# Two hybrid blocks on one core: narrow attention products given all of TensorE's rows, meta values taken once per head pair, and the squares of a norm gathered in one tile

## The chip, the cores and the metric

The kernel runs on one core of a Trainium2 chip. A core has five engines that run side by side, each working through its own instructions in order: TensorE (PE, matrix products; its weight loads are listed as PEld), VectorE (DVE), ScalarE (ACT), GpSimd (POOL) and SyncE (SP), which here only issues DMAs. They wait for each other by semaphores. Products go to PSUM, a small memory that is given out here in eight banks of 128 x 512 numbers; everything else lies in SBUF, 128 partitions wide. A matrix product takes a stationary operand of up to 128 rows by 128 columns and streams a moving one of up to 512 columns through it; the rows are the partitions over which it sums. The metric is the time of the whole program on the device in microseconds; lower is better.

## The reference, cut to what matters

Two transformer-like blocks run one after the other on 512 tokens of width 1024, all in 32-bit floats. The first block has a recurrent branch (a state-space model in chunks), an attention branch and a feed-forward part; the second a gated recurrent branch and a latent attention. The change touches both attentions and the norms:

```python
# first block: 16 heads of 64 in 2 key groups; a band of 128 keys and 16 meta tokens
s_band = einsum('bnqkgd,bnskd->bnkgqs', qb, kband) * scale + bias_band
s_meta = einsum('bnqkgd,bmkd->bnkgqm', qb, k_meta) * scale + bias_m
p = softmax(concatenate([s_meta, s_band, sink], -1), -1)
out = (einsum('bnkgqm,bmkd->bnqkgd', p_meta, v_meta)
       + einsum('bnkgqs,bnskd->bnqkgd', p_band, vband))
# second block: 8 heads, keys of 128 own numbers and 64 rotated ones that all heads share
s = (einsum('bqhd,bkhd->bhqk', qn, k_nope)
     + einsum('bqhr,bkr->bhqk', qp, k_pe)) * scale
# every norm
y = x * rsqrt(mean(x * x, axis=-1) + EPS)
```

## The kernel before, in words

**Layout.** Activations lie transposed: channels on the partitions, tokens in the free dimension. A weight tile of 128 x 1024 arrives by one DMA of 512 KB (`wload`), ScalarE copies it to a shortened form (`whi`, type fp32r) and VectorE takes the rest (`wlo`). The activations are split likewise (`split_hl`). A product of two such pairs is three products, high by high, high by low and low by high (`gemm`, lines 88 to 90), on 128 rows, in half-tokens of 256 to 264 columns in the first block and in 512 columns in the second.

**First block.** `first_mixer` goes over four groups of the recurrent branch. Each has a tile of B, one of C, four tiles x and four z; `pair_a` and `pair_b` work on a pair of heads. While a group runs, the convolution tiles of the next group (`conv_tile`, the list `jobs`), and in the last group the keys, values and queries of the attention, are put between the pairs, and so are the four output tiles of the group before (`branch`, the list `br`). `group_end` sums the squares of the group that is finished and makes the row of its norm.

**Its attention.** `attention` works on eight pairs of heads, one head of each key group on 64 partitions. `kx` is the keys laid out for four blocks of 128 queries (144 columns for the first, 272 for the others, the 16 meta keys among them). `kh[k]` holds the high part of head k's keys on both halves of the partitions, `qx[k]` the high part of its queries on one half and the low part on the other, so that one product of 128 rows (line 596) gives high by high and low by high. The third, high by low, is line 597: 64 rows of `qx` and the same 64 of `kl`, which holds the low parts of both heads, one above the other. VectorE adds the bias and takes the maximum out of PSUM (line 598), ScalarE the exponential, VectorE the scaling. `values` turns the weights round by transposes (lines 621, 633 and 637), and collects the output in one PSUM bank `pv`: for each of four query blocks first the meta values (line 640: `vm`, 32 rows, of both heads, by 128 columns), then the bands (lines 644 and 645, 64 columns of output for each head). After every head pair `self.fill` puts in other projections.

**Second block.** `Block2.run` first makes the gated recurrent branch (`hgrn_a`, `hgrn_b`), between whose heads it puts the list `jobs` of `lora_jobs`: two tiles of the key latent and three of the query latent, each with squares for its norm. Then eight heads of attention: `mla_split` divides keys and queries into high and low, `mla_a` projects the next head's, `mla_b` makes scores, softmax and transposes, `mla_c` the values. In `mla_b` the 64 rotated numbers come as one product of 128 rows (line 1137: `qx` has high and low query parts, `kph` the high key part on both halves) and one of 64 rows (line 1138: the high query part by `kpl`, the low key part). Which half of `qx` holds the high part depends on the head being even or odd. Line 1139 adds the causal mask.

**Sums of squares.** `SumSq` takes tile after tile. ScalarE squares (line 153). From the third on, the second of two kept tiles is added to the first by POOL (line 147), before a new square is made, so that two are left at the end, and `sums` (line 163) sums both over the partitions by products with a column of ones, each in two passes. There are nine such norms (four groups, the feed-forward's, two at the start of the second block, two latents) and a closing one, which is taken in two halves.

**Order.** The program text gives each engine's work; the framework's scheduler, which runs its own estimate of the engines, lays the final order of each engine's instructions and gives out buffers (a tile with the same tag waits for the earlier ones of that tag, `bufs` at a time). PSUM has tags g, a, t and o with 3, 2, 2 and 1 banks in the first block and the feed-forward, 2, 3, 2 and 1 in the second.

Of the kernel before, what the change touches and what calls it, by code (L numbers as in the profile page):

```python
# [12 lines left out]
F32 = mybir.dt.float32  # L13
F32R = mybir.dt.float32r
# [4 lines left out]
ALU = mybir.AluOpType  # L19
# [114 lines left out]
class SumSq:  # L134


    def __init__(self, g, pool, rows, nchunk, ntok, tag="ssq", bufs=1, sqtag="sq", sqbufs=2):
        self.g, self.pool, self.rows, self.nchunk, self.ntok = g, pool, rows, nchunk, ntok
        self.tag, self.bufs, self.sqtag, self.sqbufs = tag, bufs, sqtag, sqbufs
        self.parts = []  # L140

    def add(self, src, scale=None):
        nc = self.g.nc
        w = self.rows * self.nchunk
        if len(self.parts) == 2:
            a, sq = self.parts
            nc.gpsimd.tensor_tensor(a[:, :self.ntok], a[:, :self.ntok], sq[:, :self.ntok], ALU.add)  # L147
            self.parts = [a]
        tag, bufs = (self.sqtag, self.sqbufs) if self.parts else (self.tag, self.bufs)
        sq = self.pool.tile([128, w], F32, name="sq", tag=tag, bufs=bufs)  # L150
        if w > self.ntok:
            nc.gpsimd.memset(sq[:, self.ntok:], 1.0)
        nc.scalar.activation(sq[:, :self.ntok], src, AF.Square, **({} if scale is None else {"scale": scale}))  # L153
        self.parts.append(sq)

# [53 lines left out]
class Mixer:  # L209
# [288 lines left out]
    def attention(self, wk, nfill):  # L498
# [4 lines left out]
        kx = wk.tile([128, 960], F32, name="kx", tag="kx")  # L503
# [9 lines left out]

        half = (slice(0, 64), slice(64, 128))
        kh = [wk.tile([128, 960], F32R, name=f"kh{k}", tag=f"kh{k}") for k in range(2)]
        kl = wk.tile([128, 960], F32R, name="kl", tag="kl")
        for k in range(2):
            r = half[k]
            nc.scalar.activation(kh[k][r, :], kx[r, :], AF.Copy)
            nc.vector.tensor_tensor(kl[r, :], kx[r, :], kh[k][r, :].bitcast(F32), ALU.subtract)  # L520
            nc.vector.tensor_copy(kh[k][half[1 - k], :], kh[k][r, :].bitcast(F32))
# [51 lines left out]
        def scores(j):  # L573
# [17 lines left out]
            for b in range(4):  # L591
                for k in range(2):
                    n = 272 if b else 144
                    keys, cols = slice(KO[b], KO[b + 1]), slice(b * 128, (b + 1) * 128)
                    ps = psum(g, "a")
                    nc.tensor.matmul(ps[:, :n], qx[k][:, cols], kh[k][:, keys], start=True, stop=False)
                    nc.tensor.matmul(ps[:, :n], qx[k][half[k], cols], kl[half[k], keys], start=False, stop=True)  # L597
                    nc.vector.tensor_tensor_reduce(
                        out=lay(b, k), in0=ps[:, :n], in1=(bias if b else bias0)[:, k, :], scale=1.0,
                        scalar=sink[:, 2 * j + k:2 * j + k + 1], op0=ALU.add, op1=ALU.max, accum_out=mx[:, b, k:k + 1])  # L600
# [14 lines left out]
        def values(j, s):  # L615
# [8 lines left out]
            pv = psum(g, "o")  # L624
            for b in range(4):
# [14 lines left out]
                nc.tensor.matmul(pv[:, cols], vm, ptm[:, cols], start=(b == 0), stop=False)  # L640
# [39 lines left out]
def first_mixer(g, h1):  # L680

    nc, tc = g.nc, g.tc
    with ExitStack() as ctx:
# [4 lines left out]
        with tc.tile_pool(name="ssd", bufs=1, side="right", reuse_waits="tile") as wk, \  # L688
# [6 lines left out]
            for gi in range(4):  # L695
# [5 lines left out]
                for i in range(4):  # L701
                    parts = m.pair_a(wk, gi, i)
                    if prev:
                        m.pair_b(wk, *prev)
                        if i == 0:
                            br = m.group_end(wk, gi - 1)
                    prev = (gi, i, parts)
                    k = (len(jobs) + 3 - i) // (4 - i) if gi == 3 else (2 if jobs else 0)
                    m.fills = jobs[:k] + br[:1]
                    jobs, br = jobs[k:], br[1:]  # L710
                    m.fill(99)
# [99 lines left out]
class Block2:  # L811
# [191 lines left out]
    def lora_jobs(self):  # L1003
# [3 lines left out]
        self.lat, self.rl, self.mz = {}, {}, {}  # L1007

        def part(name, first, i, n, gname):
            if i == 0:  # L1010
                self.lat[name] = []
                self.ss = SumSq(g, self.wk, 128, 4, NX, "ssqa", 1, "ssqb", 1)
            t = self.t("lt")
            self.mulR(t, self.win(first + i), self.R)
# [5 lines left out]
            if i == n - 1:  # L1020
                self.rl[name] = self.ss.rstd(128.0 * n, gname)

        def kpe():
# [6 lines left out]
            self.kpe = (self.t("R1", dt=F32R, name="kph"), self.t("lt", dt=F32R, name="kpl"))  # L1030
            split_hl(g, k, *self.kpe)
# [15 lines left out]
        self.gate = gate  # L1047
        return j, kpe, norm
# [55 lines left out]
    def mla_split(self, h, kn, qn):  # L1104
# [7 lines left out]
        pr = slice((h % 2) * 64, (h % 2) * 64 + 64)  # L1112
        pl = slice(64 - (h % 2) * 64, 128 - (h % 2) * 64)
        nc.scalar.activation(qx[pr, :], qpe[pr, :], AF.Copy)
        nc.vector.tensor_tensor(qx[pl, :], qpe[pr, :], qx[pr, :].bitcast(F32), ALU.subtract)
        return kn2, qn2

    def mla_b(self, h, parts):
# [4 lines left out]
        pr = slice((h % 2) * 64, (h % 2) * 64 + 64)  # L1123
# [6 lines left out]
        def soft(b):  # L1130
# [7 lines left out]
            nc.tensor.matmul(ps[:, :n], qx[pr, qs], kpl[pr, :n], start=False, stop=False)  # L1138
# [37 lines left out]
    def run(self, r1, r12):  # L1176
# [6 lines left out]
        for h in range(8):  # L1183
# [9 lines left out]
            if 1 <= h < 6:  # L1193
                jobs.pop(0)()
# [11 lines left out]
    def output(self):  # L1206
# [30 lines left out]
        ssq = [SumSq(g, self.wk, 128, 2, HN, f"at{i}", 1, ("o", "ki")[i]) for i in range(2)]  # L1237
# [266 lines left out]
```

## Time and profile before

| what | value |
|---|---|
| median of 3 runs | 1845.95 us (1844.37 to 1847.08) |
| the profiled execution | 1847.94 us, its span 1846.1 us |
| TensorE busy, weight loads | 1802.4 us (98%), 1611.1 us (87%) |
| VectorE, ScalarE, POOL busy | 1134.4, 749.3, 299.4 us |
| granted TensorE clock | 0.994 of full |
| DMA | 158.35 MB, mean 86 GB/s |

The span is the time from the first to the last instruction of one profiled execution; the timed runs are without a profile. A row of the order of time has the start, the duration (both us), the engine, the line, the operation, the tiles (out<-in), and the shape: rows*columns of the stationary operand for a product, then its output's size, with rows first. A row of a group has the count, the busy time and the mean duration of one in ns. Matmuls overlap, so a duration of one is longer than the distance to the next one's start.

### The profile page before, as it was taken

To read this page: it belongs to the slowest core of one execution; us is meant where nothing else is said; L and a number is where in the kernel's file an instruction comes from. 1 tells how busy PE (TensorE), PEld (TensorE's weight loads), DVE (VectorE), ACT (ScalarE), POOL (GpSimd) and SP (SyncE) were. 2 spreads that over 40 slices of the span, in tenths; PEclk is the share of its full clock that TensorE was granted. 3 is DMA by queue.
4 is the path that set the end of the run, shared out by engine and by line. 5 is a ranking of instruction groups with operands and counts; after the bars stand their busy time and mean duration, and the time that the engine had idled before them with its cause. 6 is when DMAs were issued, how large, how long until landed. Compare 5 with 4: busy or idle time off the path is not lost.

```text
span 1846.1 us, 30045 instructions
## 1 busy us (share of the span) xinstructions
PE 1802.4 (98%) x12198; PEld 1611.1 (87%) x12198; DVE 1134.4 (61%) x2140; ACT 749.3 (41%) x1322; POOL 299.4 (16%) x307
## 2 busy tenths in 40 slices
PE   7999999999899999999999999999999999999997
PEld 7989999999888889999999988878888867788886
DVE  7897777844576646456666633577665466743453
ACT  4444444422344443334444433563433434532232
POOL 2344344522320001200000011100000121000113
PEclk9999999999999999999999999999999999999999
DMA  4323222222221113222222222222222121122222
GB/s 140 104 82 100 94 96 93 93 92 93 88 69 65 62 57 116 92 91 91 90 90 90 88 95 94 86 92 69 69 74 87 66 71 48 69 80 94 100 84 76
DMA packets 51310, 158.35 MB, mean 86 GB/s; under 512 B 5922, under 2 KB 9764, under 8 KB 51172
## 3 DMA queue, kind: packets, MB, share of 16 engines
q1 hardware_dynamic: 49252, 153.91, 24.5%
q10 hardware_dynamic: 1872, 2.39, 0.4%
q8 instruction: 96, 1.57, 0.3%
q14 instruction: 42, 0.34, 0.1%
q0 software_dynamic: 48, 0.13, 0.0%
HBM read 152.93 MB, written 2.16 MB: 84 GB/s over the span
## 4 chain that ended last, share of the span: by engine, by line
PE 88%; DVE 5%; ACT 2%; issue 2%; DMA 1%; POOL 1%; SPq 0%; DVEq 0%; POOLq 0%; ACTq 0%
PE ps_g L88 22%; PE ps_g L89 22%; PE ps_g L90 22%; PE ps_g L800 2%; PE ps_g L802 2%; PE ps_g L801 2%; DMA E<-csd 1%; PE ps_a L597 1%; PE ps_o L1170 1%; DVE wlo L77 1%; PE ps_a L434 1%; PE ps_t L633 1%; DVE cv L330 1%; PE ps_o L640 1%; PE ps_a L944 1%
## 5 line engine op out<-in xcount | busy, mean ns | idle before, releaser
L76 ACT ACTIVATE whi<-wraw 128x1024 fp32r<-128x1024 f32 (+2 forms) x265 | 274.9, 1038 | 607.8 <-PE ps_g L89 375.9
L77 DVE TENSOR_TENSOR wlo<-wraw,whi 128x1024 fp32r<-128x1024 f32 (+3 forms) x259 | 340.1, 1314 | 157.3 <-ACT whi L76 156.8
L88 PE MATMUL ps_g<-uh,whi 128*128 128x264 f32 (+2 forms) x1056 | 306.4, 290 | 2.5 <-DVE z L180 1.4
L89 PE MATMUL ps_g<-ul,whi 128*128 128x264 f32 (+2 forms) x1056 | 303.7, 288 | 0.0
L90 PE MATMUL ps_g<-uh,wlo 128*128 128x264 f32 (+2 forms) x1056 | 302.8, 287 | 0.0
L88 PEld LDWEIGHTS ps_g<-uh,whi 128*128 128x128 f32 x1056 | 200.6, 190 | 7.0 <-DVE z L180 1.7
L89 PEld LDWEIGHTS ps_g<-ul,whi 128*128 128x128 f32 x1056 | 200.4, 190 | 2.1
L90 PEld LDWEIGHTS ps_g<-uh,wlo 128*128 128x128 f32 x1056 | 200.5, 190 | 1.7 <-issue 0.3
L88 PE MATMUL ps_g<-fh,whi 128*128 128x256 f32 (+1 forms) x704 | 199.2, 283 | 0.8 <-DVE fx L180 0.8
L89 PE MATMUL ps_g<-fl,whi 128*128 128x256 f32 (+1 forms) x704 | 199.7, 284 | 0.0
L90 PE MATMUL ps_g<-fh,wlo 128*128 128x256 f32 (+1 forms) x704 | 199.3, 283 | 0.0
L88 PE MATMUL ps_g<-vh,whi 128*128 128x512 f32 x464 | 185.9, 401 | 0.0
L89 PE MATMUL ps_g<-vl,whi 128*128 128x512 f32 x464 | 184.4, 397 | 0.0
L90 PE MATMUL ps_g<-vh,wlo 128*128 128x512 f32 x464 | 183.9, 396 | 0.0
L88 PEld LDWEIGHTS ps_g<-fh,whi 128*128 128x128 f32 x704 | 133.3, 189 | 1.0 <-DVE fx L180 1.0
L90 PEld LDWEIGHTS ps_g<-fh,wlo 128*128 128x128 f32 x704 | 133.7, 190 | 0.0
L89 PEld LDWEIGHTS ps_g<-fl,whi 128*128 128x128 f32 x704 | 133.7, 190 | 0.0
L147 POOL TENSOR_TENSOR sq<-sq 128x514 f32<-128x514 f32 (+2 forms) x39 | 49.6, 1282 | 440.9 <-ACT sq L153 440.9
L90 PEld LDWEIGHTS ps_g<-vh,wlo 128*128 128x128 f32 x464 | 87.3, 188 | 18.9
L89 PEld LDWEIGHTS ps_g<-vl,whi 128*128 128x128 f32 x464 | 87.3, 188 | 18.5
L88 PEld LDWEIGHTS ps_g<-vh,whi 128*128 128x128 f32 x464 | 87.4, 188 | 18.1
L88 PE MATMUL ps_g<-yh,whi 128*128 128x258 f32 (+1 forms) x256 | 75.5, 295 | 1.1 <-DVE bt L471 1.1
(431 smaller groups left out, 3848.5 us busy)
## 6 DMA issues: line engine op xcount, KB each, us to landing
wraw<-in_w_in SPq DMA_DIRECT2D x128, 512.0 KB, 3.2
wraw<-in_w_ffn_in SPq DMA_DIRECT2D x44, 512.0 KB, 3.2
E<-csd SPq DMA_DIRECT2D x32, 265.0 KB, 3.9
wraw<-in_w_ssd SPq DMA_DIRECT2D x16, 512.0 KB, 3.3
wraw<-in_w_out SPq DMA_DIRECT2D x16, 512.0 KB, 3.2
wraw<-in_w_ffn_out SPq DMA_DIRECT2D x16, 512.0 KB, 3.2
wraw<-in_w_pab SPq DMA_DIRECT2D x16, 512.0 KB, 3.2
wraw<-in_w_att SPq DMA_DIRECT2D x8, 512.0 KB, 3.2
```

What stands on the lines that cost most here:

```text
L76: nc.scalar.activation(hf[:, :n], raw[:, :n], AF.Copy)
L77: (eng or nc.vector).tensor_tensor(lf[:, :n], raw[:, :n], hf[:, :n].bitcast(F32), ALU.subtract)
L88: nc.tensor.matmul(ps, wh, a, start=(i == 0), stop=False)
L89: nc.tensor.matmul(ps, wh, b, start=False, stop=False)
L90: nc.tensor.matmul(ps, wl, a, start=False, stop=(i == last))
L147: nc.gpsimd.tensor_tensor(a[:, :self.ntok], a[:, :self.ntok], sq[:, :self.ntok], ALU.add)
L330: nc.vector.scalar_tensor_tensor(cv, xr[:, j:j + NT], w(j), cv, ALU.mult, ALU.add)
L434: nc.tensor.matmul(yd[k * 64:k * 64 + 64, (c - c0) * CH:(c - c0 + 1) * CH], xd[:CH, c, k * 64:k * 64 + 64], Es[k][:CH, c * CH:(c + 1) * CH ...
L597: nc.tensor.matmul(ps[:, :n], qx[k][half[k], cols], kl[half[k], keys], start=False, stop=True)
L800: nc.tensor.matmul(ps, wh, uh, start=(k == 0), stop=False)
L801: nc.tensor.matmul(ps, wh, ul, start=False, stop=False)
L802: nc.tensor.matmul(ps, wl, uh, start=False, stop=(k == NFF - 1))
```

## The change

- **Line 597:** `kl` becomes two tiles, one per head, each with the low part on its own half and zeros on the other. The product runs on 128 rows. `kx` gives up its own buffer and takes one of the two of tag `s`.
- **Line 640:** one product of 512 columns stands ahead of the four query blocks, in place of one of 128 in each.
- **Line 1138:** `kpl` keeps its lower half and gets zeros in the upper one; `qx` always has the high part below and the low part above, for an odd head by one ScalarE copy more. The product runs on 128 rows.
- **`SumSq`:** the addition on POOL follows each square at once, so that one tile is left for `sums`. The closing norm keeps the old way (`keep=True`). The padding column is set only in the first tile.
- **Order:** a convolution tile of the next group (in the last group the attention's keys) goes between the first pair and `group_end`; the sums of a latent wait for the projection of the next tile, and one job is added for the last.

```diff
 class SumSq:
...
     def add(self, src, scale=None):
         nc = self.g.nc
         w = self.rows * self.nchunk
-        if len(self.parts) == 2:
-            a, sq = self.parts
-            nc.gpsimd.tensor_tensor(a[:, :self.ntok], a[:, :self.ntok], sq[:, :self.ntok], ALU.add)
-            self.parts = [a]
+        if self.keep:
+            self.gather()
         tag, bufs = (self.sqtag, self.sqbufs) if self.parts else (self.tag, self.bufs)
         sq = self.pool.tile([128, w], F32, name="sq", tag=tag, bufs=bufs)
-        if w > self.ntok:
+        if w > self.ntok and not self.parts:
             nc.gpsimd.memset(sq[:, self.ntok:], 1.0)
         nc.scalar.activation(sq[:, :self.ntok], src, AF.Square, **({} if scale is None else {"scale": scale}))
         self.parts.append(sq)
+        if not self.keep:
+            self.gather()
+
+    def gather(self):
+        if len(self.parts) == 2:
+            a, sq = self.parts
+            self.g.nc.gpsimd.tensor_tensor(a[:, :self.ntok], a[:, :self.ntok], sq[:, :self.ntok], ALU.add)
+            self.parts = [a]
...
-        kx = wk.tile([128, 960], F32, name="kx", tag="kx")
+        kx = wk.tile([128, 960], F32, name="kx", tag="s", bufs=2)
...
-        kl = wk.tile([128, 960], F32R, name="kl", tag="kl")
+        kl = [wk.tile([128, 960], F32R, name=f"kl{k}", tag=f"kl{k}") for k in range(2)]
         for k in range(2):
-            r = half[k]
+            r, z = half[k], half[1 - k]
+            nc.gpsimd.memset(kl[k][z, :].bitcast(F32), 0.0)
             nc.scalar.activation(kh[k][r, :], kx[r, :], AF.Copy)
-            nc.vector.tensor_tensor(kl[r, :], kx[r, :], kh[k][r, :].bitcast(F32), ALU.subtract)
-            nc.vector.tensor_copy(kh[k][half[1 - k], :], kh[k][r, :].bitcast(F32))
+            nc.vector.tensor_tensor(kl[k][r, :], kx[r, :], kh[k][r, :].bitcast(F32), ALU.subtract)
+            nc.vector.tensor_copy(kh[k][z, :], kh[k][r, :].bitcast(F32))
...
-                    nc.tensor.matmul(ps[:, :n], qx[k][half[k], cols], kl[half[k], keys], start=False, stop=True)
+                    nc.tensor.matmul(ps[:, :n], qx[k][:, cols], kl[k][:, keys], start=False, stop=True)
...
             pv = psum(g, "o")
+            nc.tensor.matmul(pv, vm, ptm, start=True, stop=False)
             for b in range(4):
...
-                nc.tensor.matmul(pv[:, cols], vm, ptm[:, cols], start=(b == 0), stop=False)
...
                         m.pair_b(wk, *prev)
                         if i == 0:
+                            jobs.pop(0)()
                             br = m.group_end(wk, gi - 1)
...
-                    k = (len(jobs) + 3 - i) // (4 - i) if gi == 3 else (2 if jobs else 0)
+                    k = (len(jobs) + 3 - i) // (4 - i) if gi == 3 else 1 if i == 0 and gi else (2 if jobs else 0)
...
         def part(name, first, i, n, gname):
+            ps = self.win(first + i)
             if i == 0:
                 self.lat[name] = []
+                sums()
                 self.ss = SumSq(g, self.wk, 128, 4, NX, "ssqa", 1, "ssqb", 1)
...
             if i == n - 1:
-                self.rl[name] = self.ss.rstd(128.0 * n, gname)
+                self.last = (name, 128.0 * n, gname)
+
+        def sums():
+            if self.last:
+                name, width, gname = self.last
+                self.rl[name] = self.ss.rstd(width, gname)
+            self.last = None
...
-            self.kpe = (self.t("R1", dt=F32R, name="kph"), self.t("lt", dt=F32R, name="kpl"))
-            split_hl(g, k, *self.kpe)
+            kph = self.t("R1", dt=F32R, name="kph")
+            nc.scalar.activation(kph, k, AF.Copy)
+
+            kpl = self.t("lt", dt=F32R, name="kpl")
+            nc.gpsimd.memset(kpl[64:128, :].bitcast(F32), 0.0)
+            nc.vector.tensor_tensor(kpl[0:64, :], k[0:64, :], kph[0:64, :].bitcast(F32), ALU.subtract)
+            self.kpe = (kph, kpl)
...
+        j.append(sums)
...
-        pr = slice((h % 2) * 64, (h % 2) * 64 + 64)
-        pl = slice(64 - (h % 2) * 64, 128 - (h % 2) * 64)
-        nc.scalar.activation(qx[pr, :], qpe[pr, :], AF.Copy)
-        nc.vector.tensor_tensor(qx[pl, :], qpe[pr, :], qx[pr, :].bitcast(F32), ALU.subtract)
+        lo, up = slice(0, 64), slice(64, 128)
+        src = up if h % 2 else lo
+        nc.scalar.activation(qx[lo, :], qpe[src, :], AF.Copy)
+        if h % 2:
+            nc.scalar.activation(qx[up, :], qpe[up, :], AF.Copy)
+        nc.vector.tensor_tensor(qx[up, :], qpe[src, :], qx[src, :].bitcast(F32), ALU.subtract)
...
-            nc.tensor.matmul(ps[:, :n], qx[pr, qs], kpl[pr, :n], start=False, stop=False)
+            nc.tensor.matmul(ps[:, :n], qx[:, qs], kpl[:, :n], start=False, stop=False)
...
-            if 1 <= h < 6:
+            if 1 <= h < 7:
                 jobs.pop(0)()
...
-        ssq = [SumSq(g, self.wk, 128, 2, HN, f"at{i}", 1, ("o", "ki")[i]) for i in range(2)]
+        ssq = [SumSq(g, self.wk, 128, 2, HN, f"at{i}", 1, ("o", "ki")[i], keep=True) for i in range(2)]
```

More of the change, by code (lines that the diff above doesn't have):

```diff
@@ L134, with __init__ @@
 class SumSq:
-    def __init__(self, g, pool, rows, nchunk, ntok, tag="ssq", bufs=1, sqtag="sq", sqbufs=2):
-        self.g, self.pool, self.rows, self.nchunk, self.ntok = g, pool, rows, nchunk, ntok
+    def __init__(self, g, pool, rows, nchunk, ntok, tag="ssq", bufs=1, sqtag="sq", sqbufs=2, keep=False):
+        self.g, self.pool, self.rows, self.nchunk, self.ntok, self.keep = g, pool, rows, nchunk, ntok, keep
         self.tag, self.bufs, self.sqtag, self.sqbufs = tag, bufs, sqtag, sqbufs
@@ L1006, in lora_jobs @@
         base = 32
-        self.lat, self.rl, self.mz = {}, {}, {}
+        self.lat, self.rl, self.mz, self.last = {}, {}, {}, None
         def part(name, first, i, n, gname):
+            ps = self.win(first + i)
             if i == 0:
                 self.lat[name] = []
+                sums()
                 self.ss = SumSq(g, self.wk, 128, 4, NX, "ssqa", 1, "ssqb", 1)
             t = self.t("lt")
-            self.mulR(t, self.win(first + i), self.R)
+            self.mulR(t, ps, self.R)
             hi = self.t("lf", dt=F32R)
@@ L1122, in mla_b @@
         qx, (kph, kpl) = self.qx, self.kpe
-        pr = slice((h % 2) * 64, (h % 2) * 64 + 64)
         scale = 192.0 ** -0.5
```

## The prediction

> **What bounds the kernel now.** I read the page first, then the busy times by stage, then the order of time on TensorE.
>
> ```profile
> span 1846.1 us, 30045 instructions
> PE 1802.4 (98%) x12198; PEld 1611.1 (87%) x12198; DVE 1134.4 (61%) x2140; ACT 749.3 (41%) x1322; POOL 299.4 (16%) x307
> PE 88%; DVE 5%; ACT 2%; issue 2%; DMA 1%; POOL 1%; SPq 0%; DVEq 0%; POOLq 0%; ACTq 0%
> ```
>
> TensorE is busy for 98% of the span and holds 88% of the chain of waits. A busy share can hide slow instructions, so the stages of the change are looked at singly: the first block's attention (540 to 700 us), the second block's (1480 to 1630), and for comparison the first block's recurrent part (20 to 500).
>
> ```profile
> core 0: us, PE busy (x) PEld busy (x) DVE busy (x) ACT busy (x) POOL busy (x), PEclk, DMA share, GB/s
> 540.00:700.00 160.00, 160.00 (x1195) 133.84 (x1193) 90.46 (x260) 80.26 (x203) 0.15 (x1) 1.00 0.21 70
> 1480.00:1630.00 150.00, 146.08 (x681) 110.46 (x680) 103.30 (x224) 71.26 (x205) 16.19 (x8) 0.99 0.20 64
> 20.00:500.00 480.00, 467.29 (x4012) 457.12 (x4010) 347.87 (x626) 197.90 (x301) 175.91 (x195) 0.99 0.28 93
> ```
>
> In the first attention TensorE never idles, at full clock, while VectorE has 69.5 us and ScalarE 79.7 us to spare and the DMA engines stand at 0.21. So what an instruction takes of TensorE's time there, from its start to the next one's start, is time of the kernel. The durations in the rows overlap (matmuls are pipelined); I use the distance of starts only.
>
> **Part A, the low products of the first attention (line 597).** They contract 64 rows; the change lets them contract 128, half of them zeros.
>
> ```profile
> 559.86 0.29 PE L596 MATMUL ps_a<-kh,qx 128*128 128x272 f32 x1
> 560.08 0.39 PE L597 MATMUL ps_a<-kl,qx 64*128 64x272 f32 x1
> 560.39 0.38 PE L89 MATMUL ps_g<-ul,whi 128*128 128x256 f32 x1
> 560.62 0.28 PE L90 MATMUL ps_g<-uh,wlo 128*128 128x256 f32 x1
> 560.74 0.28 PE L88 MATMUL ps_g<-uh,whi 128*128 128x256 f32 x1
> 511.48 0.33 PE L597 MATMUL ps_a<-kl,qx 64*128 64x144 f32 x1
> 511.74 0.33 PE L596 MATMUL ps_a<-kh,qx 128*128 128x144 f32 x1
> 512.01 0.33 PE L597 MATMUL ps_a<-kl,qx 64*128 64x144 f32 x1
> ```
>
> Between full-row products a start follows the last one by 0.12 us (560.62 to 560.74), so four take 0.48. The four from 559.86 to 560.74, with one 64-row product among them, take 0.88, 0.40 us more than their columns need: 0.22 instead of 0.12 goes by before it starts, 0.31 while it runs, 0.23 on the one behind it. The 144-column pair takes 0.53 (511.48 to 512.01) where two full-row products of 128 columns would take 0.22 (0.11 each, below): 0.31 more.
>
> ```profile
> L597 PE MATMUL ps_a<-kl,qx 64*128 64x272 f32 x48 | 18.7, 389 | 0.0
> L597 PE MATMUL ps_a<-kl,qx 64*128 64x144 f32 x16 | 5.3, 331 | 0.0
> ```
>
> 48 x 0.40 + 16 x 0.31 = 24.2 us. Some low products stand beside other narrow ones, where part of the price stays; I take 23. The ends are 17, if the 0.11 on the product behind belongs to that one (48 x 0.29 + 16 x 0.20), and 25.
>
> **Part B, the low product of the second attention (line 1138).**
>
> ```profile
> 1617.09 0.27 PE L1135 MATMUL ps_a<-kh,ql 128*128 128x128 f32 x1
> 1617.20 0.28 PE L1136 MATMUL ps_a<-kl,qh 128*128 128x128 f32 x1
> ...
> 1618.02 0.31 PE L1137 MATMUL ps_a<-kph,qx 128*128 128x128 f32 x1
> 1618.25 0.32 PE L1138 MATMUL ps_a<-kpl,qx 64*128 64x128 f32 x1
> 1618.51 0.23 PE L1139 MATMUL ps_a<-amask,identb 128*128 128x128 bf16 x1
> 1618.55 0.48 PE L90 MATMUL ps_g<-vh,wlo 128*128 128x512 f32 x1
> 1618.87 0.40 PE L88 MATMUL ps_g<-vh,whi 128*128 128x512 f32 x1
> 1619.10 0.39 PE L89 MATMUL ps_g<-vl,whi 128*128 128x512 f32 x1
> L1138 PE MATMUL ps_a<-kpl,qx x32: 322/410/502, 1491.2 to 1618.3; 64*128 64x512 f32 x8, 64*128 64x384 f32 x8, 64*128 64x256 f32 x8, 64*128 64x128 f32 x8
> ```
>
> Four products take 0.85 us (1618.02 to 1618.87). At full rows they would take 0.11 three times and 0.23: 0.56, so 0.29 is the price, 9.3 us over 32. No row shows the bf16 mask product without a 64-row one ahead of it; were its own change of type the cause of what follows it, only 0.12 + 0.15 ahead of 1618.51 would be won (8.6), and were the mask product worth only the 0.04 of its row, 0.36 (11.5). I take 9.3.
>
> **Part C, the meta values.** Four products of 128 columns on 32 rows a head pair (two passes each) become one of 512.
>
> ```profile
> 564.17 0.48 PE L640 MATMUL ps_o<-ptm,vm 32*128 32x128 f32 x2
> 564.58 0.43 PE L645 MATMUL ps_o<-pt,vtok 128*64 128x128 f32 x2
> L640 PE MATMUL ps_o<-ptm,vm 32*128 32x128 f32 x64 | 15.5, 321 | 0.0
> 1614.87 1.67 PE L1170 MATMUL ps_o<-pT,vt 128*128 128x512 f32 x4
> 1616.37 0.82 PE L1170 MATMUL ps_o<-p,vt 128*128 128x256 f32 x4
> ```
>
> Old: 32 times 0.41 (564.17 to 564.58) = 13.1. A pass of this kind streams at 1.50 us for 2 x (512 + 384) columns (1614.87 to 1616.37), 0.84 ns a column, so 0.43 for 512; with the old product's surplus of 0.10 a pass (0.205 against 0.107 for 128 columns) the new one takes 2 x 0.53 = 1.06, 8.5 over eight head pairs. 4.6 is left. The 64-column products beside it will now pay some of the changeover themselves: I take 4, ends 3 and 7 (the latter if entering three times less saves 0.1 each).
>
> **Part D, the sums of squares.** The last square is now added on POOL, so one tile instead of two goes through TensorE.
>
> ```profile
> 791.67 0.98 PE L163 MATMUL ps_t<-ones,sq 128*103 128x1 f32 x10
> 1416.58 1.68 PE ps_t L163 x16
> ```
>
> One tile is 10 products in about 0.9 us (five norms: four groups and the feed-forward's), or 8 of the 16 that took 1.68, 0.84 (four: two at the second block's input, two latents): 4.5 + 3.4 = 7.9. The closing norm keeps its two tiles. It costs nine more POOL additions, and before each the sums must wait:
>
> ```profile
> 783.59 1.87 POOL L147 TENSOR_TENSOR sq<-sq 128x514 f32<-128x514 f32 x1 [3.77 <-ACT sq L153]
> 788.68 0.62 ACT L153 ACTIVATE sq<-h 128x514 f32<-128x514 f32 x1
> 1156.09 2.56 POOL L147 TENSOR_TENSOR sq<-sq 128x512 f32<-128x512 f32 x2 [12.84 <-ACT sq L153]
> 1497.25 0.63 ACT L1114 ACTIVATE qx<-vf 64x512 fp32r<-64x512 f32 x1
> ```
>
> At the feed-forward's start the last square ends at 789.30 and the sums stand 2.37 us behind it; an addition of 1.3 to 1.9 us fits in between. At the second block's input two additions in a row take 2.56. In the groups a whole convolution tile now stands between, and the latents' sums move behind the next projection; these cover 1.3 us wherever TensorE has them queued. Cover gone, each of the nine costs at most 1.9, 17 in all. I take 2.
>
> **Small moves.** The zero fills (two of 64 x 960, one of 64 x 512) go to POOL, which is idle for 304 of the 480 us in the third stage row and 134 of 150 in the second; the two thinner halves of kpl and the shared buffer of kx take no more instructions than before. An odd head of the second attention gains one ScalarE copy (0.63, the last row above), on the way from its qpe to line 1137; four of them, at most 2.5 us, I take 1.
>
> **What is late next.** With TensorE some 27 us shorter in the first attention, 160 us become about 133, and VectorE's 90.5 us are 68% of it. The recurrent stage runs VectorE at 72% (347.87 of 480) and leaves TensorE idle for 12.7 us, 2.6%. By that 2.6% of 133, 3.5 us, comes back as waits; ends 0 and 14 (below).
>
> **Sum.** 23 + 9.3 + 4 + 7.9 = 44.2 off; 2 + 1 + 3.5 = 6.5 on; net 37.7. The profiled execution took 1847.94 us (1.8 outside its span), so 1810.2; it lies 2.0 over the median of the three timed runs, 1845.95, so **1808** there. With all bounds at their good ends and no waits, 25 + 11.5 + 7 + 7.9 = 51.4: 1795. At their bad ends, 17 + 8.6 + 3 + 7.9 - 17 - 2.5 - 14 = 3, which asks for all at once; half of the waits (17) gives 1826.
>
> **Rivals.**
>
> *The price is not one of the rows* (0.06). A low product might be slow because its weights, the ones of the product just before it, cannot be loaded while that one runs. Then A and B win nothing, D and C stay: 1846 - 11.9 + 3 = 1837. Against it: lines 88 and 89 use the same weights too, stand 0.12 apart, and the surplus appears at 64 and 32 rows alike. The Trainium skill ("TensorE: Matmul & The Clock Gate", Part 3) says a weight load overlaps a running matmul only when their row groups differ, which, taken literally, would give this case; the full-row rows 0.12 us apart speak against that reading.
>
> *VectorE takes over in the first attention* (0.13). TensorE's queue is in order; a score product must wait until VectorE has emptied one of two score buffers.
>
> ```profile
> L598 DVE CUSTOM_DVE_ANT_0 s<-ps_a,bias,par 128x272 f32<-128x272 f32 (+1 forms) x64 | 29.3, 463 | 31.9 <-PE ps_a L597 25.2 <-PE ps_t L633 6.3
> 128.75 2.79 POOL xe L384
> ```
>
> Now VectorE waits for TensorE there, 25.2 us. If that turned and each of 64 score products waited 0.22 us, 14 us of 27 would be lost: 1808 + 11 beyond the 3.5 already in = 1819. It decides from the point at which two filled score buffers stand behind other work on VectorE.
>
> *The additions hold up POOL* (0.03), the one on the other side. POOL is in order too; an addition placed before its square is there holds back the products xe and E behind it, and TensorE's line 403 waits for xe. The longest such step on the chain is 2.79 us; at each of 16 head pairs it is 45: 1808 + 45 = 1853. It needs POOL to reach the addition some 3 us early every time; POOL's 37% load in that stage and only one addition more per group of four pairs speak against.
>
> *Something of equal size gives it all back* (0.03): the order of all engines is laid anew, and about 38 us more of idle appear; the stage rows show no such slackness.
>
> **Chances.** Forecast 0.75, with its own range 1796 to 1826; rivals as given. Range 1796 to 1829. A measurement of this kernel tells about 0.2% (3.7 us) from no change; faster 0.94, same 0.03, slower 0.03.
>
> **What will show it.** The low products at 128 rows, starting 0.12 us apart from their neighbours; if they still take 0.3, A and B are wrong. Line 640's group with 16 products of 512 columns, 0.5 us apart. 98 products for sums instead of 180, 48 additions instead of 39. The first attention shorter by some 24 us net and the second by 8 to 9; if TensorE idles over 5 us in the first, the second rival has part of it. Line 403's wait for xe grown by over 10 us would be the third.

## The result and the profile after

The changed kernel takes **1819.36 us** (median; 1816.29 to 1820.97) where the kernel before takes 1846.51 in the same comparison: a ratio of 0.9849, interval 0.9836 to 0.9861, or 27.2 us less by the medians. The forecast was 1808, 38 us less, in a range of 1796 to 1829. Two executions of the series, one of the kernel before and one of the kernel with the latents' sums back and the meta product on 128 rows, took 6389.85 and 5492.65 us and are left out of every number below. The page of the changed kernel:

```profile
span 1814.5 us, 29816 instructions
PE 1760.9 (97%) x12068; PEld 1588.9 (88%) x12068; DVE 1135.3 (63%) x2140; ACT 752.0 (41%) x1326; POOL 321.8 (18%) x300
PE 84%; DVE 7%; ACT 3%; issue 2%; POOL 2%; DMA 2%; SPq 0%; DVEq 0%; POOLq 0%; ACTq 0%
```

TensorE's share of the chain fell from 88% to 84%, VectorE's rose from 5% to 7%. TensorE is busy 41.5 us less (1802.4 to 1760.9), but what it is not busy grew by 9.9: span less busy time is 1846.1 - 1802.4 = 43.7 before and 1814.5 - 1760.9 = 53.6 after. The mean granted clock is 0.992 after against 0.994, which is 14.5 us lost (0.008 of the span) against 11.1, so 3.4 of the busy time that is left is a slower clock. The work itself fell by 41.5 + 3.4 = 44.9 us; 44.2 were forecast. (The clock is given to 0.001, so each of the two losses is known to 0.9 us.)

The low products of the first attention and one meta product, in the order of time of the changed kernel (start and duration in us):

```profile
561.42 0.29 PE L605 MATMUL ps_a<-kl,qx 128*128 128x272 f32 x1
561.54 0.29 PE L604 MATMUL ps_a<-kh,qx 128*128 128x272 f32 x1
561.67 0.29 PE L605 MATMUL ps_a<-kl,qx 128*128 128x272 f32 x1
561.80 0.28 PE L88 MATMUL ps_g<-uh,whi 128*128 128x258 f32 x1
...
606.14 0.28 PE L89 MATMUL ps_g<-ul,whi 128*128 128x256 f32 x1
606.35 1.12 PE L633 MATMUL ps_o<-ptm,vm 32*128 32x512 f32 x2
607.40 0.44 PE L653 MATMUL ps_o<-pt,vtok 128*64 128x128 f32 x4
```

The groups of the changed instructions in the same kernel (count | busy us, mean ns of one | idle before):

```profile
L605 PE MATMUL ps_a<-kl,qx 128*128 128x272 f32 x48 | 13.8, 291 | 0.0
L633 PE MATMUL ps_o<-ptm,vm 32*128 32x512 f32 x16 | 9.0, 640 | 0.0
L169 PE MATMUL ps_t<-ones,sq 128*128 128x1 f32 x48 | 5.8, 240 | 0.1
L169 PE MATMUL ps_o<-ones,sq 128*103 128x1 f32 x40 | 4.0, 223 | 0.0
L169 PE MATMUL ps_t<-ones,sq 128*103 128x1 f32 x10 | 1.0, 223 | 0.0
L159 POOL TENSOR_TENSOR sq<-sq 128x514 f32<-128x514 f32 (+2 forms) x48 | 61.9, 1298 | 499.1 <-ACT sq L151 499.1
```

The low products now start 0.12 to 0.13 us after their neighbours and the one behind follows at the same distance: the 0.40 us of surplus is gone. The meta product takes 1.05 us for its two passes (606.35 to 607.40; 1.06 worked out). There are 48 + 40 + 10 = 98 products for sums and 48 additions on POOL, as worked out.

What TensorE waited for in the kernel before, by line and releaser (us in total, times, the longest):

```profile
PE ps_t L403 <- POOL xe L384: 6.4, 5, 2.6
PE ps_t L538 <- POOL vbd L535: 1.5, 1, 1.5
PE ps_a L89 <- DVE ul L62: 1.2, 2, 1.0
PE ps_o L129 <- DVE rq_y L112: 1.2, 1, 1.2
PE ps_g L1074 <- ACT vt L1077: 0.2, 1, 0.2
```

The same view of the changed kernel:

```profile
PE ps_t L409 <- POOL xe L390: 6.0, 5, 2.7
PE ps_o L129 <- DVE rq_y L112: 4.7, 3, 1.9
PE ps_g L1097 <- ACT vt L1100: 4.4, 2, 4.1
PE ps_g L88 <- ACT ah L58: 1.2, 1, 1.2
PE ps_t L129 <- DVE rq_y L112: 0.9, 1, 0.9
```

Three waits are new or grown: the row of a norm (line 129: 1.2 to 4.7 + 0.9), the evacuation of `vt` in the second block's values (0.2 to 4.4), and the attention's end (`ah`, 1.2). All three lie where the change moved sums or laid the order anew.

**The 4.1 us wait in detail**, the order of time of the changed kernel, engine by engine (line 1079 and 1080 are the key's rotation, 1048 the high part `kph`, 1100 empties the values' bank):

```profile
1432.80 1.69 POOL L1079 TENSOR_TENSOR lf<-lf,kk 128x512 f32<-128x512 f32 x1 [53.94 <-DMA th<-lf]
1434.46 2.36 POOL L77 TENSOR_TENSOR wlo<-wraw,whi 128x1024 fp32r<-128x1024 f32 x1
...
1434.53 2.84 DVE L1080 TENSOR_TENSOR lf<-lf,th 128x512 f32<-128x512 f32 x1 [1.16 <-POOL lf L1079]
...
1437.40 0.63 ACT L1048 ACTIVATE kph<-lf 128x512 fp32r<-128x512 f32 x1 [3.17 <-DVE lf L1080]
...
1439.32 0.67 ACT L1100 ACTIVATE vt<-ps_g,rq_y 128x512 f32<-128x512 f32 x1
...
1435.55 0.40 PE L1099 MATMUL ps_g<-wlo,lf 128*128 128x512 f32 x1
1440.04 0.79 PE L1097 MATMUL ps_g<-whi,lf 128*128 128x512 f32 x1 [4.09 <-ACT vt L1100]
1440.63 0.63 PE L1098 MATMUL ps_g<-whi,kk 128*128 128x512 f32 x1
1441.06 0.63 PE L1099 MATMUL ps_g<-wlo,lf 128*128 128x512 f32 x1
```

The sums of the latents come one job later, and the values' projection starts before the key's rotation is through. ScalarE works in order: the copy to `kph` waits 3.17 us for VectorE's addition and stands ahead of the evacuation that TensorE needs. Here that is the second `vt`; the first was emptied at 1433.54. In the kernel before, the rotation's addition (1458.70) and the copy (1459.41) were done before the first `vt` was emptied (1463.86); its order of time:

```profile
1458.70 0.68 DVE L1057 TENSOR_TENSOR lf<-lf,th 128x512 f32<-128x512 f32 x1
...
1463.86 0.70 ACT L1077 ACTIVATE vt<-ps_g,rq_y 128x512 f32<-128x512 f32 x1
```

Behind the wait the products of 512 columns start 0.43 us apart (1440.63 to 1441.06) instead of 0.23: TensorE's granted clock is 0.53 from 1440 to 1443.4, and 1.00 again behind that. Stretches of the changed kernel (us; busy time and count of each engine; then the granted clock):

```profile
core 0: us, PE busy (x) PEld busy (x) DVE busy (x) ACT busy (x) POOL busy (x), PEclk, DMA share, GB/s
500.00:504.00 4.00, 3.49 (x17) 3.33 (x18) 3.17 (x6) 2.96 (x5) 0.07 (x1) 0.64 0.00 0
540.00:700.00 160.00, 158.37 (x1317) 142.97 (x1318) 98.37 (x266) 83.56 (x201) 6.50 (x5) 1.00 0.26 84
1430.00:1445.00 15.00, 10.57 (x41) 7.99 (x40) 6.86 (x7) 7.05 (x13) 4.02 (x2) 0.89 0.08 19
```

The clock is low behind these waits (500 to 504, from some 2 us behind the end of the 1.9 us of line 129; 1430 to 1445), while in the first attention it is full and TensorE idles for 1.63 us only. A half-clock stretch lasts some 3.4 us and so loses 1.7. Read in windows of 2 us, the profile before has four of them (in 32 to 36, 130 to 136, 530 to 534 and 1500 to 1504 us) and that of the changed kernel six (in 500 to 506, 522 to 526, 770 to 774, 1440 to 1444 and two in a row in 1474 to 1482), and in both the clock is low in the last 10 us, where TensorE is mostly idle. The two stretches more come to the 3.4 us of clock between the two profiles.

### The profile page after: what moved, and what is told of

It is laid out like the page before. It is cut to its first block, busy times and chain, and to the rows that moved or that the text cites. A ratio compares the mean times of both kernels' runs of the same rounds, so it can differ in the third digit from the quotient of the medians.

```text
span 1814.5 us, 29816 instructions
## 1 busy us (share of the span) xinstructions
PE 1760.9 (97%) x12068; PEld 1588.9 (88%) x12068; DVE 1135.3 (63%) x2140; ACT 752.0 (41%) x1326; POOL 321.8 (18%) x300
## 4 chain that ended last, share of the span: by engine, by line
PE 84%; DVE 7%; ACT 3%; issue 2%; POOL 2%; DMA 2%; SPq 0%; DVEq 0%; POOLq 0%; ACTq 0%
PE ps_g L88 22%; PE ps_g L90 22%; PE ps_g L89 22%; PE ps_g L810 2%; PE ps_g L809 2%; PE ps_g L811 2%; DVE wlo L77 1%; DVE cv L336 1%; PE ps_o L1194 1%; DMA E<-csd 1%; PE ps_t L642 1%; PE ps_a L953 1%; POOL xe L390 1%; PE ps_a L440 1%; PE ps_t L409 1%
## 5 line engine op out<-in xcount | busy, mean ns | idle before, releaser
L77 DVE TENSOR_TENSOR wlo<-wraw,whi 128x1024 fp32r<-128x1024 f32 (+3 forms) x259 | 335.0, 1294 | 151.7 <-ACT whi L76 151.0
L88 PE MATMUL ps_g<-fh,whi 128*128 128x258 f32 (+1 forms) x704 | 199.9, 284 | 0.8 <-DVE fx L186 0.8
L159 POOL TENSOR_TENSOR sq<-sq 128x514 f32<-128x514 f32 (+2 forms) x48 | 61.9, 1298 | 499.1 <-ACT sq L151 499.1
```

Source lines behind the costliest of these rows:

```text
L77: (eng or nc.vector).tensor_tensor(lf[:, :n], raw[:, :n], hf[:, :n].bitcast(F32), ALU.subtract)
L88: nc.tensor.matmul(ps, wh, a, start=(i == 0), stop=False)
L159: self.g.nc.gpsimd.tensor_tensor(a[:, :self.ntok], a[:, :self.ntok], sq[:, :self.ntok], ALU.add)
```

## The experiments

Theory 1: the price of narrow products is one of the rows, so A (line 597) and B (line 1138) bring what was worked out, and the missing 11 us are waits that D (the sums) made, with the clock behind them. The rivals: A or B bring less than their price, as something late next in the attentions takes it back (theory 2), or the new order as a whole costs it, whichever part it comes from (theory 3). Each kernel was timed beside the kernel before; "before" is 1846.42 for the first four, 1846.38 for the next four, 1846.19 and 1847.6 for the last two pairs.

**A alone.**

```diff
-        kl = wk.tile([128, 960], F32R, name="kl", tag="kl")
+        kl = [wk.tile([128, 960], F32R, name=f"kl{k}", tag=f"kl{k}") for k in range(2)]
...
+            nc.gpsimd.memset(kl[k][z, :].bitcast(F32), 0.0)
...
-                    nc.tensor.matmul(ps[:, :n], qx[k][half[k], cols], kl[half[k], keys], start=False, stop=True)
+                    nc.tensor.matmul(ps[:, :n], qx[k][:, cols], kl[k][:, keys], start=False, stop=True)
```

> The kernel before with part A alone (line 597 on 128 rows beside zeros). Theory 1 (TensorE's savings are as costed, and the waits that ate 10 us of them belong to the moved sums of part D): 20 to 23 us off, 1823 to 1826, low products 0.12 to 0.13 us from their neighbours, no new idle in the first attention. Theory 2 (the waits come because a shorter attention runs into VectorE and ScalarE): only 10 to 15 us off, 1831 to 1836, and more than 5 us of idle on TensorE between 540 and 700 us.

1822.68 us, ratio 0.9869 (0.9855 to 0.9883), so 24.2 us off; 23 were forecast. The first attention of this kernel, same columns as above:

```profile
540.00:700.00 160.00, 160.00 (x1336) 146.50 (x1335) 99.21 (x266) 84.42 (x201) 6.50 (x5) 1.00 0.25 81
```

TensorE does not idle at all there. Nothing becomes late in this stage when 24 us of its work go.

**B alone.**

```diff
-            nc.tensor.matmul(ps[:, :n], qx[pr, qs], kpl[pr, :n], start=False, stop=False)
+            nc.tensor.matmul(ps[:, :n], qx[:, qs], kpl[:, :n], start=False, stop=False)
```

(with `kpl`, its zeros and `qx` as in the change)

> The kernel before with part B alone (line 1138 on 128 rows, the halves of qx always in one order, the odd heads' extra copy). Theory 1: 8 to 9 us off, 1837 to 1838. Theory 2: 3 to 5 us off, because the heads' queries are not ready earlier and TensorE waits for their low part (2.3 us already, before the second product of a head).

1840.39 us, 0.9959 (0.9947 to 0.9971), so 7.6 off (5.4 to 9.8). 9.3 less the 1 for the odd heads' copy were forecast. The order of time of B alone shows the mask product behind a full-row one:

```profile
1606.21 0.28 PE L1144 MATMUL ps_a<-kpl,qx 128*128 128x256 f32 x1
1606.33 0.23 PE L1145 MATMUL ps_a<-amask,identb 128*128 128x128 bf16 x1
1606.37 0.48 PE L88 MATMUL ps_g<-yhi,whi 128*128 128x512 f32 x1
1606.69 0.39 PE L88 MATMUL ps_g<-vh,whi 128*128 128x512 f32 x1
```

The mask product now starts 0.12 us behind the low product. But from the product after the mask to the next it is still 0.32 us (1606.37 to 1606.69), as in the kernel before (1618.55 to 1618.87), where full-row products of 512 columns otherwise stand 0.23 apart. So that part of the price goes with the bf16 mask product, and what B saves is the 0.12 + 0.15 ahead of it in the prediction's rows: 0.27 a product, 8.6 in all. Less the 1 for the copy, which no run shows by itself, that is the 7.6 measured.

**C alone.**

```diff
             pv = psum(g, "o")
+            nc.tensor.matmul(pv, vm, ptm, start=True, stop=False)
             for b in range(4):
...
-                nc.tensor.matmul(pv[:, cols], vm, ptm[:, cols], start=(b == 0), stop=False)
```

> The kernel before with part C alone (one meta product of 512 columns per head pair). Both theories: 3 to 5 us off, 1841 to 1843; the two passes 0.53 and 0.52 us long. That less than 2 us come off would say that the products beside it now pay the change of the rows.

1846.55 us, 1.0002 (0.9991 to 1.0014): nothing, where 4 were forecast. The 16 passes are as long as worked out (9.0 us in the group of 512 columns above), but the attention's end shows this, in the order of time of C alone:

```profile
684.28 0.40 PE L645 MATMUL ps_o<-pt,vtok 128*64 128x128 f32 x4
686.73 0.62 PE L88 MATMUL ps_g<-ah,whi 128*128 128x258 f32 x3 [2.05 <-ACT ah L58]
...
688.40 0.42 PE L89 MATMUL ps_g<-al,whi 128*128 128x258 f32 x1
688.62 0.42 PE L90 MATMUL ps_g<-ah,wlo 128*128 128x258 f32 x1
```

In the new order the projections that fill the attention are used up before its end, and the output projection has to wait 2.05 us for the last head pair's `ah`; from 688.2 on the products start 0.22 us apart instead of 0.12.

**D alone.**

```diff
+        if not self.keep:
+            self.gather()
...
+                            jobs.pop(0)()
                             br = m.group_end(wk, gi - 1)
...
-                self.rl[name] = self.ss.rstd(128.0 * n, gname)
+                self.last = (name, 128.0 * n, gname)
...
+        j.append(sums)
```

> The kernel before with part D alone (the last square added on POOL, the sums behind a convolution tile or the next projection). Theory 1: TensorE does 7.9 us less, and some 8 to 12 us of new waits stand ahead of line 129 and in the values' projection of the second block, so no gain: 1843 to 1850. Theory 2: 6 to 8 us off, 1838 to 1840, with no such waits.

1852.72 us, **1.0032** (1.0021 to 1.0043): slower by 5.9. What TensorE waited for in D alone:

```profile
PE ps_o L129 <- DVE rq_y L112: 4.7, 3, 1.9
PE ps_g L1091 <- ACT vt L1094: 3.6, 2, 3.3
PE ps_a L89 <- DVE ul L62: 2.3, 2, 1.3
PE ps_g L88 <- ACT ah L58: 2.1, 1, 2.1
PE ps_t L129 <- DVE rq_y L112: 0.9, 1, 0.9
```

All the new waits of the changed kernel are here, without A, B or C. Against the rows of before they are 4.4 (line 129) + 3.4 (`vt`) + 1.1 (`ul`) + 2.1 (`ah`) = 11.0 longer, less 1.5 for `vbd`, which is gone. TensorE's busy time fell by 8.6 us (1802.4 to 1793.8), and its idle time rose by 9.1 (43.7 to 1846.6 - 1793.8 = 52.8). In the profiled execution the two nearly cancel; at 1848.39 us it is the fastest of this kernel. Others reach 1857.99, with granted clocks from 0.994 down to 0.989.

**Everything but D, and A with B.** The first is the change with `SumSq`, the convolution tile and the latents as before, the second the first with:

```diff
-            nc.tensor.matmul(pv, vm, ptm, start=True, stop=False)
             for b in range(4):
...
+                nc.tensor.matmul(pv[:, cols], vm, ptm[:, cols], start=(b == 0), stop=False)
```

> The changed kernel without part D (parts A, B and C on the kernel before). Theory 1 (part D costs more in waits than it saves, also beside A to C): the parts alone add up to 1846.4 - 24.2 - 7.6 + 0.1 = 1814.7, so 4 to 5 us under the changed kernel, 1813 to 1816. Theory 3 (the loss of D alone was the luck of one order, and the changed kernel's shortfall comes from elsewhere): 1819 to 1824.

> Parts A and B alone, the meta values as before. If part C's saving (TensorE's start distances say some 4 us) only fell to a wait that one order put at the attention's end: 2 to 4 us over the run with A, B and C, 1816 to 1819. If it is worth nothing wherever it stands: the same as that run within 1 us.

A, B and C: 1815.94, 0.9836 (0.9820 to 0.9852). A and B: 1815.33, 0.9829 (0.9816 to 0.9842). By the medians the change without D is 3.4 us faster than with it (the intervals overlap from 0.9836 to 0.9852), and C adds nothing to A and B.

**The latents' sums back at their place**, the rest as changed.

```diff
-            ps = self.win(first + i)
...
-            self.mulR(t, ps, self.R)
+            self.mulR(t, self.win(first + i), self.R)
...
-                self.last = (name, 128.0 * n, gname)
+                self.rl[name] = self.ss.rstd(128.0 * n, gname)
...
-        j.append(sums)
...
-            if 1 <= h < 7:
+            if 1 <= h < 6:
```

> The changed kernel with the two latents' sums back where they were (right behind the last square, with the addition on POOL kept). Theory 1: the wait of 4.3 us in the values' projection of the second block and the slow clock behind it go: 1812 to 1815. Theory 3: within 1.5 us of the changed kernel, 1818 to 1821.

1811.91, 0.9821 (0.9803 to 0.9838): 7.5 us less than the changed kernel by the medians, 5.2 by the ratios, whose intervals overlap from 0.9836 to 0.9838 only. The wait for the evacuation is gone, in the view of TensorE's waits:

```profile
PE ps_g L1094 <- ACT vt L1097: 0.2, 1, 0.2
```

The two latents still go through TensorE as one tile each; it was not the gathering that cost, but the later place of the sums.

**The groups' sums as before**, the rest as changed.

```diff
-            self.ssq = SumSq(g, wk, ROWS, 5, NO)
+            self.ssq = SumSq(g, wk, ROWS, 5, NO, keep=True)
...
-                            jobs.pop(0)()
                             br = m.group_end(wk, gi - 1)
```

> The changed kernel with the four groups' sums as before (two tiles through TensorE, no convolution tile ahead of them). Theory 1: TensorE does 3.6 us more, the waits ahead of line 129 at 165, 267 and 497 us (1.8, 1.3 and 0.7 more than before) go, and at most one fall of the clock: 1816 to 1820. Theory 3: 3 to 4 us slower, 1822 to 1824.

1815.81, 0.9835 (0.9823 to 0.9848): 3.5 less than the changed kernel by the medians, with intervals that overlap. Line 129's wait in `ps_o` is back at 1.2 us.

**D only at the feed-forward's norm and the second block's two** (both edits above together), with C and without.

> The changed kernel with the groups' and the latents' sums as before, so that of part D only the feed-forward's norm and the two norms at the second block's input remain. Theory 1 (each place of part D costs its own wait, and the two places undone singly gave 7.5 and 3.6 us): 1807 to 1811. If the places are not independent (the same falls of the clock were counted twice): 1811 to 1815.

> The same without part C. In the run with part C alone TensorE waits 2.2 us at the end of the first attention, where before a half projection stood; without it this projection stands there again. If C's saving falls to that wait: the same as the run with A, B, C within 2 us, 1807 to 1813, with no wait before the projection of the attention's output. If C does save in this order: 3 to 4 us slower than that run.

With C 1811.7, 0.9813 (0.9799 to 0.9826); without 1816.26, 0.9837 (0.9824 to 0.9851). With C it was to be the best by the sum of the two edits, 7.5 + 3.5; it is no better than the first edit alone. But it is 4.2 us below A, B and C without any of D (1815.94), by the medians, with intervals that overlap. So the gathering at the three norms whose sums kept their place, 0.9 + 2 x 0.84 = 2.6 us of TensorE by the prediction's count, seems to pay. Here C is worth 4.6 us by the medians (the intervals overlap from 0.9824 to 0.9826), though the profiled execution without it is the shorter one (span 1811.8 against 1813.0). By time alone the runs on C disagree.

**The meta product on 128 rows too**, in the kernel with the latents' sums back, and in the one with both sums back and C.

```diff
-        vm = wk.tile([32, 128], F32, name="vm", tag="vm")
+        vm = wk.tile([128, 128], F32, name="vm", tag="vm")
+        nc.gpsimd.memset(vm, 0.0)
+        ptms = [wk.tile([128, 512], F32, name=f"ptm{k}", tag=f"ptm{k}") for k in range(2)]
+        for t in ptms:
+            nc.gpsimd.memset(t, 0.0)
...
-            nc.vector.tensor_copy(ptm, pm[:32, :])
+            nc.vector.tensor_copy(ptm[:32, :], pm[:32, :])
```

> The changed kernel with the latents' sums where they were, and the meta product, too, on 128 rows (96 of them zeros, set once in vm and in two tiles of weights). Theory 1 (the price belongs to the rows, whatever their number): its two passes come 0.43 us apart instead of 0.53, the product behind it no longer pays, some 0.3 to 0.4 us per head pair or 3 us in all: 1808 to 1810. If the 32 rows are not what costs: the same as the run with the latents' sums put back, 1811 to 1813, passes still 0.53.

> The same meta product in the kernel that also has the groups' sums as before. Theory 1: 1808 to 1810; if the 32 rows are not what costs: 1811 to 1813.

With the latents' sums back: **1806.46**, 0.9779 (0.9767 to 0.9792), the fastest of all and 13 us under the changed kernel. In the other: 1809.0, 0.9788 (0.9775 to 0.9801). The product's group and one head pair of the first in the order of time:

```profile
L637 PE MATMUL ps_o<-ptm,vm 128*128 128x512 f32 x16 | 8.2, 592 | 0.0
...
607.92 0.28 PE L90 MATMUL ps_g<-uh,wlo 128*128 128x258 f32 x1
608.04 1.02 PE L637 MATMUL ps_o<-ptm,vm 128*128 128x512 f32 x2
608.99 0.43 PE L657 MATMUL ps_o<-pt,vtok 128*64 128x128 f32 x2
```

It starts 0.12 us behind a full-row product and takes 0.95 to the next, where the changed kernel's took 0.21 and 1.05. That is 0.19 for each of eight head pairs, 1.5 us where 3 were expected, of the 5.5 and 2.7 us between the medians; the table below puts 0.4 and 1.5 us down to the work and 4.7 and 1.9 to the clock.

**Work and clock apart.** Every execution comes with its mean granted clock. Span times clock is what the span would be at full clock if all of it went with TensorE, and the rest of the span is what the clock lost: a rough split, since the clock is given to 0.001 (0.9 us either way in one execution) and is low at the end of the kernel too, where TensorE mostly idles. The value at full clock scatters by 0.6 to 2.0 us between executions of one kernel (standard deviation), and most kernels have four or five, so a difference of 1 us between two rows says nothing. Median of the first, mean of the second, over the executions compared:

| kernel | median time | at full clock | lost to the clock |
|---|---|---|---|
| before | 1846.42 | 1833.2 | 11.4 |
| A | 1822.68 | 1810.7 | 10.9 |
| B | 1840.39 | 1826.4 | 12.1 |
| C | 1846.55 | 1830.6 | 13.8 |
| D | 1852.72 | 1834.9 | 15.9 |
| A, B | 1815.33 | 1803.1 | 10.5 |
| A, B, C | 1815.94 | 1801.4 | 13.4 |
| all: the changed kernel | 1819.36 | 1800.5 | 16.8 |
| latents back | 1811.91 | 1795.6 | 15.2 |
| groups back | 1815.81 | 1800.5 | 13.4 |
| both back | 1811.70 | 1798.5 | 12.3 |
| both back, no C | 1816.26 | 1801.3 | 12.7 |
| latents back, meta product on 128 rows | 1806.46 | 1795.2 | 10.5 |
| both back, meta product on 128 rows | 1809.00 | 1797.0 | 10.4 |

In this split C saves 2.6, 1.7 and 2.8 us at full clock in its three comparisons (alone; with A and B; with D at three norms), which is its 4.6 less the 2.1 us wait; the clock takes 2.4 and 2.9 of that back in two of them and 0.4 the other way in the third. That would explain why the times disagree. The kernel with three gathered norms (both back) is 2.9 us under A, B and C at full clock, which fits the 2.6 counted. Groups back: at full clock nothing changes, as four sums of 0.9 us come back and 3.5 us of waits go; by the split the gain of 3.5 is all clock. D as a whole, in the changed kernel, is worth 0.9 at full clock (1801.4 to 1800.5) and loses 3.4 to the clock.

## Why the prediction was right or wrong

**Right: the prices on TensorE.** Part A was forecast at 23 and alone is 24.2, which is 48 x 0.40 + 16 x 0.31 without the 1.2 taken off for narrow neighbours. The low end of 17 gave the 0.11 us to the product behind; the rows 0.12 to 0.13 us apart show that it belonged to the narrow one. Part B was forecast at 9.3 less 1 and is 7.6. Its low bound of 8.6, less the 1, was the right one, and for the reason given with it: the mask product has a price of its own. The counts of part D came out, and its 7.9 us are 8.6 in D's busy time. All of TensorE's work fell by 44.9 against 44.2, as near as the clock lets it be told.

**Wrong: the term for the waits**, 2 + 1 + 3.5 = 6.5. In the profiled executions 9.9 us of idle and 3.4 us of clock came on. The step that failed is the one that costs D's moved sums: "these cover 1.3 us wherever TensorE has them queued", so 2 was taken between 0 and 17. It looked at the addition of 1.3 us alone, and not at what the moved sums, or the convolution tile put ahead of them, make late. D alone shows 9.1 us more idle. In the latents it is the rotation's copy ahead of the `vt` evacuation in ScalarE's queue; putting the sums back takes the wait away, and 7.5 us by the medians with it. In the groups it is the norm's row. In the first, TensorE's sums end 1.1 us earlier than before (155.19 against 156.29), but VectorE takes the first step towards the row 2.8 us later (line 107: 159.36 against 156.60), behind two steps of the convolution tile that now stands ahead (line 336, from 156.81); TensorE waits 1.67 us where it did not wait. In the last one TensorE stops at the same distance behind its sums as before, 4.45 us (492.44 to 496.89; 497.11 to 501.56), but VectorE's eleven short steps from line 107 to the last of line 112 now take from 492.48 to 498.65 instead of from 497.58 to 502.61, with other VectorE work between them. The prediction asked what a late addition holds up in POOL's queue (its third rival), and did not ask the same of ScalarE's and VectorE's. Where the sums kept their place, D brought about what was counted (2.9 us at full clock against 2.6).

**Wrong in size: "what is late next".** 3.5 us were put on the first attention because it would become as tight as the recurrent stage. With A alone the idle is 0, in the changed kernel 1.63 of 160. An average of another stage said nothing of this one. In its place, C's and D's new orders each put a wait of 2.1 us at the attention's end, which a count of instructions could not show: the order of all engines is laid anew with each edit.

**Wrong in size: C.** Its passes were right and the time was not: 0 at the median against 4, by that wait and, as the split has it, the clock.

**Not in the sum at all: the clock.** A wait on TensorE was costed by its own length. The table puts the loss at 11.4 us before and 16.8 after, so 5.4 of the difference. By the split, the forecast of 38 less meets 32.7 at full clock, and the clock takes it to 27. Which part made that loss is shown only in part: the stretch behind 1440 is D's, while the one near 500 comes in A alone and C alone too.

**The rivals.** That the price is not one of the rows falls with A alone, and with the meta product, which got faster with more rows. That VectorE takes over falls with A's 160.00 of 160 us busy; VectorE is at 99.2 there. That this rival's price, 1819, is the time measured is luck: the 11 us were lost elsewhere. That the additions hold up POOL, the one on the slower side, falls as a whole: line 403, 409 now, waits 6.0 us for `xe` against 6.4. Yet the part it spoke of did end on the slower side when done alone, by other queues. Of the 38 us that the last rival gives back, 11 came back. The profiled execution before lay 1.4 us above the later median, and the one after 3.1 below its own, so that the two traces differ by 31.6 us and the medians by 27.2.

## What to carry to other kernels

Where TensorE never idles, price a product on fewer rows by the distance of starts from the full-row product ahead of it to the one behind it; here a 64-row one cost 0.40 us more than a full one, and zeros in the other rows won it back. A step that saves TensorE some tenths of a microsecond by giving another engine work, or by moving its result, should be followed through every in-order queue it passes, and a wait it makes should be costed with the clock behind it (here 1.7 us a stretch, behind some waits and not behind others). As far as these runs tell, such savings were worth their count where the result stayed in its place, and nothing or less where it was moved. When an edit saves a few microseconds, time its parts singly, for the new order is part of the edit.

## What the runs showed of the hardware

**The clock after short waits.** A wait of 1.9 us (before 498.80 in the changed kernel) or 2.05 (C alone) was followed, 1.5 to 2.2 us behind its end, by about 3.3 us at half clock, 688.2 to 691.4 in C alone, where products of 256 or 258 columns started 0.22 us apart. The Trainium skill ("TensorE: Matmul & The Clock Gate", Part 1) puts the drop after at least one idle window of about 3.4 us; the length of the stretch agrees with such a window, but no wait of that length stood ahead of these two. Whether a wait is followed by such a stretch varies from trace to trace. At the last group's norm the 1.2 us wait was followed by one in 7 of the 10 traces that have it (not in the kernel before, B alone, and A with B) and the 1.9 us wait in all 4; the wait of 2.6 to 2.7 us for `xe` near 130 us in 8 of 14. C alone ran from 1842.31 us to 1853.27, with clocks from 0.995 to 0.988. What decides it was not tried.

**An addition held by another engine.** VectorE's addition of 0.68 us took 2.84 beside POOL's 2.36 us subtraction (1434.46 to 1436.82) and ended 0.55 us after that (1437.37). The Trainium skill ("SBUF — State Buffer", Who interferes with whom) says that a VectorE instruction with two SBUF inputs and a GpSimd one that reads SBUF exclude each other, the later one waiting for the whole of the earlier. These rows agree; it lengthened the 4.1 us wait, and no run took it away alone. In the first group VectorE's step of line 62 took 2.10 us (152.51 to 154.61) beside work of POOL, the last of it an addition of squares that D puts there (152.77 to 154.06); in the kernel before it took 0.86.

**Narrow products cost on both sides.** A single 64-row product among full-row ones cost 0.10 us ahead, 0.19 on itself and 0.11 behind; a 32-row one of 512 columns 0.09 ahead (0.21 against 0.12) and 0.10 over its two passes (1.05 against 0.95).
